# Column tiles in pairs, operands loaded in place, residual tiles one by one: a change to the FFN of a hybrid decoder step

## The chip, the cores and the metric

The kernel runs on one core of a Trainium2 chip. The metric is the device time of one execution in microseconds (us). The profile is that of one execution, with its time given beside its span.

## What is computed

The reference is one step of a decoder layer for 2048 prompt tokens and 32 sample tokens (width 1024): a mixer of differential attention and retention, its output added to the tokens, then a SwiGLU FFN (inner width 2816) and a final norm, all in float32. What the change touches is the FFN and the writing of its operands:

```
def swiglu(h, w_in_l, w_out_l):
    g, u = jnp.split(h @ w_in_l, 2, axis=-1)
    return (jax.nn.silu(g) * u) @ w_out_l
...
    xp = xp + swiglu(rms_norm(xp, norm_ffn_g[l], NORM_EPS), w_ffn_in[l], w_ffn_out[l])
...
y_prompt = rms_norm(xp, norm_final_g, NORM_EPS)
y_sample = rms_norm(xs, norm_final_g, NORM_EPS)
```

## The kernel before

**Arithmetic.** A float32 product is made of three matmuls: each operand is split into a high part (a cast on ACT, L122) and a low part (source minus high part on DVE, L123), and TensorE (PE) adds high times high, low times high and high times low. The FFN's block products use a scheme of seven products for a 2 by 2 block multiplication, with sums of blocks in place of the eighth. The products have the numbers 0, 4, 5, 6, 1, 2, 3, in the order in which they are run.

**Mixer's output.** For each tile of 128 tokens the output stage (`stats`, `weigh`, `finish`, `sums`, L957 to L1013) writes the residual x to DRAM (x2_d, which the profile calls x_d), norms and transposes the tile (ctp, L979), and writes blocks of it as xop_d: blocks 0, 1 and 3 directly (L993 to L996), blocks 4, 6, 5 and 2 after four sums of a pair of tiles on POOL (L1008 to L1013). SP issues these writes. xop_d[g][o] holds the operand of product o for token half g (g = 0, 1; 1024 tokens each). The sample tokens go to xs_d.

**FFN-in** (`ffn_in`, L1075 to L1233) runs over the token halves g, in each over eleven pairs of column tiles j, in each over the two tiles e of the pair.
- `operands(g)` (L1095) loads 28 blocks of 256 KB, four (k) for each product. A load goes into one of four staging buffers so0 to so3, and is split from there into the tiles xh and xl of that product and k. There is one such tile each, so those of g = 1 wait for the last product of g = 0 that reads them. POOL's sums at the end of a pair (L1215 to L1218) use the same four buffers.
- For each tile e SP loads 1 MB of w (L1178, two buffers, also used by w2); `weights` (L1109) makes four differences on POOL (wt) and splits seven halves into wh and wl, which have eight buffers each.
- `product` (L1133) runs 12 matmuls of 128 by 128 by 512 into one PSUM bank (fps, L1139). Seven banks go around, and four are taken for each e: products 0 and 1 share one, 4 and 2, 6 and 3, and 5 has its own.
- Between them ACT copies banks (c1, c5), DVE adds a bank to a line (L1191, L1194, L1203, L1207), and ACT applies silu.
- In g = 0 the sample tokens take part (`sample_in` L1148: sz, DVE's copy zs, then strips at L1167). They need xs, which POOL loads at L1089.
- At the end of a pair POOL makes four sums and writes seven blocks hop_d of 256 KB (L1221).
- In g = 1 `second` (L1235) follows: SP loads w2 (two rows of w_ffn_out, L1239), PE multiplies the sample tokens with it (sacc, L1243), and POOL writes four differences top_d (L1258).

**FFN-out** (`ffn_out`, L1260 to L1353) runs the seven products in the order 0, 1, 5, 4, 2, 6, 3, each over eleven j and eight PSUM banks p. `operands` (L1290) loads hop_d (512 KB, staging xr, three buffers) and a row of w_ffn_out or top_d (256 KB, wr, four) on SP and splits them into xh, xl, vh and vl, four buffers each; a j has 24 matmuls (L1305). The 16 residual tiles x (512 KB each) are loaded on POOL at L1278, before the products. At the end of product 0 the sample rows are loaded (xsr, L1351), added to ysum (L1352) and normed.

**What sets the order.** Each engine works through one queue in order, and so do the queues on which SP and POOL issue DMAs. The framework places each engine's instructions with a model of their times, so an instruction can stand elsewhere than the program's text has it. The pools of the FFN lie on one side of the on-chip memory: a tile of FFN-out may lie where tiles of FFN-in were, and then it waits for the last reader of those.

Of the kernel before, what the change touches and what calls it, by code (L numbers as in the profile page):

```python
# [11 lines left out]
F32 = mybir.dt.float32  # L12
F32R = mybir.dt.float32r
# [8 lines left out]
P = 128  # L22
# [23 lines left out]
class Step:  # L46
# [3 lines left out]
    def run(self):  # L50
        tc = self.tc
        with (
# [11 lines left out]
            self.xs_d = dram.tile([P, KT, NS], F32, name="xs_d")  # L64
            self.hop_d = [[dram.tile([P, 2, 512], F32, name=f"hop_d{j}_{o}") for o in range(7)] for j in range(NF // 2)]
# [822 lines left out]
    def out_rows(self, cr, ps, tiles, zps=None):  # L888
# [82 lines left out]
        def finish(t):  # L971
# [24 lines left out]
            nc.sync.dma_start(d[3][:, :, c], xt[:, half:])  # L996
            self.odd = (t, xt)

        def sums():
# [12 lines left out]
            for o, src in ((4, a22), (6, a21), (5, a11), (2, a12)):  # L1012
                nc.sync.dma_start(d[o][:, :, c], src)  # L1013
# [40 lines left out]
    def ffn(self):  # L1054
        tc, nc, a = self.tc, self.nc, self.a
        with ExitStack() as st:
# [8 lines left out]
            self.ysum = fs.tile([NS, D], F32, name="ysum")  # L1065
# [9 lines left out]
    def ffn_in(self):  # L1075
        nc, tc, a = self.nc, self.tc, self.a
        half = KT // 2
        with ExitStack() as st:
# [9 lines left out]
            xs = fx.tile([P, KT, NS], F32, name="xs")  # L1088
            nc.gpsimd.dma_start(xs, self.xs_d)  # L1089
            acc = None  # L1090

            def line(tag, bufs=1):
                return fw.tile([P, 512], F32, tag=tag, name=tag, bufs=bufs)

            def operands(g):  # L1095
                x = {}
                n = 0
                for o in (0, 4, 5, 6, 1, 2, 3):
                    for k in range(half):
                        r = line(f"so{n % 4}")  # L1100
                        n += 1
                        nc.sync.dma_start(r, self.xop_d[g][o][:, k, :])
# [6 lines left out]
            def weights(w):  # L1109
                wv = w.rearrange("p s k c -> p s (k c)")  # L1110
                w11, w21, w12, w22 = wv[:, 0, :512], wv[:, 0, 512:], wv[:, 1, :512], wv[:, 1, 512:]
                ws = {}

                def put(o, src):
                    h, l = self.halves(fw, src, 512, ("wh", "wl"), 8)
                    ws[o] = (h, l)

                tt = nc.gpsimd.tensor_tensor
                put(0, w11)
                t1, t2, t3, t4 = (line("wt", 4) for _ in range(4))  # L1120
                tt(t1, w12, w11, ALU.subtract)
                put(4, t1)
                tt(t2, w22, t1, ALU.subtract)
                put(5, t2)
                tt(t3, w22, w12, ALU.subtract)
                put(6, t3)
                put(1, w21)
                put(2, w22)
                tt(t4, w21, t2, ALU.subtract)
                put(3, t4)  # L1130
                return ws

            def product(o, bank, x, ws, first):  # L1133
                h, l = ws[o]
# [13 lines left out]
            def sample_in(f, w):  # L1148
# [11 lines left out]
                zs = fw.tile([P, 2 * P], F32, tag="zs", name="zs", bufs=1)  # L1160
# [9 lines left out]

            for g in range(2):
                x = operands(g)
                for j in range(NF // 2):
                    hh = []
                    for e in range(2):
                        f = j + e * (NF // 2)
                        w = fw.tile([P, 2, KT, P], F32, tag="w", name="w", bufs=2)
                        nc.sync.dma_start(w, a["w_ffn_in"][f].rearrange("s p k c -> p s k c"))  # L1178
                        ws = weights(w)
                        ba, bb, bc_, bd = (ring.tile() for _ in range(4))  # L1180
                        product(0, ba, x, ws, True)
# [340 lines left out]
```

## Time and profile before

| | us |
|---|---|
| median of three runs | 2728.57 (2726.32 to 2728.86) |
| profiled execution | 2728.34 |
| its span | 2726.6 |
| PE busy | 2616.8 (96%) |
| DVE busy | 1568.0 (58%) |
| ACT busy | 1061.8 (39%) |
| POOL busy | 950.8 (35%) |
| mean DMA rate | 152 GB/s |

A busy PE is not PE at its best: it counts as busy at the reduced clock too, so the granted clock is read beside it. The stages of the FFN are seen by PE's lines: L1153 and L1139 begin with FFN-in at about 1338 us, L1243 marks the second token half, L1305 begins at 2281 us and ends at 2713 us.

### The profile page before, as it was taken

The page shows a single profiled execution, that of the slowest core. Times are in us where ns is not written, and L with a number is a line of the kernel's source. Part 1 is how long each engine was busy: PE and PEld are TensorE (multiplying, and loading weights), DVE is VectorE, ACT ScalarE, POOL GpSimd, SP SyncE. Part 2 cuts the span into 40 slices and gives each one's busy share as a digit, 9 for nine tenths or more (in the row PEclk, how much of TensorE's full clock was granted, in tenths as well). Part 3 has the DMA queues.
Part 4 walks back from the last instruction along what each step waited for, and adds up shares of the span by engine and source line. Part 5 has one row for each costly group of instructions (what it writes and reads, how often), then busy time and mean ns, then how long its engine had stood idle before and what let it go on. Part 6 is the DMA issues. An engine that isn't in the chain of part 4 may idle for free. (4 is left out here: it accounts for less than half of the span.)

```text
span 2726.6 us, 35659 instructions
## 1 busy us (share of the span) xinstructions
PE 2616.8 (96%) x13180; PEld 2092.6 (77%) x13180; DVE 1568.0 (58%) x2296; ACT 1061.8 (39%) x2051; POOL 950.8 (35%) x991
## 2 busy tenths in 40 slices
PE   8999999999898999998899999979999999899998
PEld 7777788787566888887667777757888787688886
DVE  5554554543657677774375555547877874345364
ACT  4343343432556555653243333334332332332342
POOL 1000000011651122214246555546777774003121
PEclk9999999999999999999999999989999999899999
DMA  7436455364995455525442233245444447544463
GB/s 248 127 102 193 142 161 144 109 178 129 271 243 136 130 166 134 145 84 177 152 139 93 82 102 107 82 147 174 142 167 139 147 163 278 175 145 146 144 203 114
DMA packets 197550, 413.12 MB, mean 152 GB/s; under 512 B 20176, under 2 KB 84368, under 8 KB 197376
## 3 DMA queue, kind: packets, MB, share of 16 engines
q1 hardware_dynamic: 133568, 265.66, 30.7%
q0 software_dynamic: 54592, 140.98, 17.5%
q10 hardware_dynamic: 9216, 4.20, 0.6%
q8 instruction: 104, 1.70, 0.3%
q14 instruction: 70, 0.57, 0.1%
HBM read 287.82 MB, written 122.95 MB: 151 GB/s over the span
## 5 line engine op out<-in xcount | busy, mean ns | idle before, releaser
L1139 PE MATMUL fps<-xh,wh 128*128 128x512 f32 x1232 | 486.9, 398 | 20.0 <-ACT xh L122 19.6
L1139 PE MATMUL fps<-xl,wh 128*128 128x512 f32 x1232 | 483.3, 393 | 3.4 <-DVE xl L123 3.4
L1139 PE MATMUL fps<-xh,wl 128*128 128x512 f32 x1232 | 481.0, 391 | 0.0
L294 PE MATMUL z<-wh,xh 128*128 128x512 f32 x768 | 303.7, 397 | 7.7 <-ACT xh L188 7.7
L296 PE MATMUL z<-wl,xh 128*128 128x512 f32 x768 | 304.2, 397 | 0.0
L295 PE MATMUL z<-wh,xl 128*128 128x512 f32 x768 | 302.4, 394 | 0.0
L1139 PEld LDWEIGHTS fps<-xh,wh 128*128 128x128 f32 x1232 | 232.5, 189 | 89.9 <-ACT xh L122 25.3
L1139 PEld LDWEIGHTS fps<-xl,wh 128*128 128x128 f32 x1232 | 232.7, 189 | 57.0 <-DVE xl L123 9.3
L1139 PEld LDWEIGHTS fps<-xh,wl 128*128 128x128 f32 x1232 | 232.6, 189 | 49.3 <-issue 0.4
L123 DVE TENSOR_TENSOR wl<-wt,wh 128x512 fp32r<-128x512 f32 x176 | 218.4, 1246 | 77.7 <-ACT wh L122 73.1
L1305 PE MATMUL ops<-vh,xh 128*128 128x512 f32 x616 | 234.1, 391 | 12.7 <-ACT xh L122 10.6
L1305 PE MATMUL ops<-vh,xl 128*128 128x512 f32 x616 | 239.3, 391 | 0.0
L1305 PE MATMUL ops<-vl,xh 128*128 128x512 f32 x616 | 239.1, 390 | 0.0
L792 DVE TENSOR_REDUCE mx<-sp 128x1 f32<-128x1024 f32 (+4 forms) x192 | 168.7, 908 | 77.5 <-PE sp L791 76.9
L123 DVE TENSOR_TENSOR wl<-w,wh 128x512 fp32r<-128x512 f32 x132 | 161.2, 1232 | 87.9 <-ACT wh L122 87.9
L122 ACT CAST wh<-w 128x512 fp32r<-128x512 f32 x132 | 81.3, 621 | 304.6 <-PE fps L1139 170.5
L122 ACT CAST wh<-wt 128x512 fp32r<-128x512 f32 x176 | 109.1, 621 | 212.3 <-PE fps L1139 174.6
L123 DVE TENSOR_TENSOR wl<-wr,wh 128x1024 fp32r<-128x1024 f32 x96 | 117.3, 1223 | 106.7 <-ACT wh L122 94.4
L294 PEld LDWEIGHTS z<-wh,xh 128*128 128x128 f32 x768 | 145.2, 189 | 37.8 <-ACT xh L188 7.7
L296 PEld LDWEIGHTS z<-wl,xh 128*128 128x128 f32 x768 | 144.7, 188 | 31.9 <-issue 0.7
L295 PEld LDWEIGHTS z<-wh,xl 128*128 128x128 f32 x768 | 144.9, 189 | 31.1 <-issue 0.3
L123 DVE TENSOR_TENSOR vl<-wr,vh 128x512 fp32r<-128x512 f32 x77 | 58.3, 759 | 187.0 <-ACT vh L122 183.8
(307 smaller groups left out, 5002.8 us busy)
## 6 DMA issues: line engine op xcount, KB each, us to landing
wr<-w_in SPq DMA_DIRECT2D x96, 512.0 KB
w<-w_ffn_in SPq DMA_DIRECT2D x44, 1024.0 KB
xr<-hop_d SPq DMA_DIRECT2D x77, 512.0 KB
hop_d<-so POOLq DMA_DIRECT2D x88, 256.0 KB, 2.7
kst<-k_d POOLq DMA_DIRECT2D x36, 512.0 KB, 6.8
hop_d<-h POOLq DMA_DIRECT2D x66, 256.0 KB, 2.3
qd<-q_d POOLq DMA_DIRECT2D x64, 256.0 KB, 5.6
xop_d<-xt SPq DMA_DIRECT2D x56, 256.0 KB
```

Source lines behind the costliest of these rows:

```text
L122: nc.scalar.copy(hi, src)
L123: nc.vector.tensor_tensor(lo, src, hi.bitcast(F32), ALU.subtract)
L294: mm(z, h[:, j, c], wh[:, j], start=k == 0, stop=False)
L295: mm(z, l[:, j, c], wh[:, j], start=False, stop=False)
L296: mm(z, h[:, j, c], wl[:, j], start=False, stop=k == KT - 1)
L792: nc.vector.tensor_reduce(mx[:, c : c + 1], sp[:, :w], AX.X, ALU.max, negate=True)
L1139: nc.tensor.matmul(bank, w[:, c], v, start=first and k == 0 and n == 0, stop=k == half - 1 and n == 2, skip_group_check=True,)
L1305: nc.tensor.matmul(bank, x[:, c], w, start=first and n == 0, stop=end and n == 2, skip_group_check=True)
```

## The change

- The mixer's blocks xop_d are written by POOL's queue instead of SP's.
- FFN-in's operands are loaded into the xl tiles themselves, and xl is replaced in place by the low part. The staging buffers so are now POOL's alone. xs is loaded after the operands of g = 0 are asked for in the text.
- The two tiles e of a pair go side by side: both w are loaded, each product is run for e = 0 and then for e = 1, and the halves of the weights are made in that order. Six banks are taken for a pair; product 5 shares one with 6 and 3. The lines u2, sg and z21 are gone, their contents going into c1, u3 and h.
- `second` stands between products 6 and 1 instead of at the end of the pair.
- ysum goes through DRAM (ys_d). Small lines get a pool of their own (fe).
- In FFN-out the operands are loaded into xl in place, and xh, xl, vh and vl have five buffers. The residual tiles are loaded on SP, a pair of them behind each of the first eight operands of product 0. The sample rows are added and normed at product 5.

The core of the diff. Of FFN-in's loop only the new lines are shown; the old ones are in the listing above.

```
+    self.ys_d = dram.tile([NS, D], F32, name="ys_d")
...
-        nc.sync.dma_start(d[0][:, :, c], xt[:, :half])
-        nc.sync.dma_start(d[1][:, :, c], xt[:, half:])
+        nc.gpsimd.dma_start(d[0][:, :, c], xt[:, :half])
+        nc.gpsimd.dma_start(d[1][:, :, c], xt[:, half:])
...
-        nc.sync.dma_start(d[o][:, :, c], src)
+        nc.gpsimd.dma_start(d[o][:, :, c], src)
...
-    self.ysum = fs.tile([NS, D], F32, name="ysum")
...
+    fe = pool("fe", bufs=1)
...
     def operands(g):
         x = {}
-        n = 0
         for o in (0, 4, 5, 6, 1, 2, 3):
             for k in range(half):
-                r = line(f"so{n % 4}")
-                n += 1
-                nc.sync.dma_start(r, self.xop_d[g][o][:, k, :])
                 h = fx.tile([P, 512], F32R, tag=f"xh{o}{k}", name=f"xh{o}{k}")
                 l = fx.tile([P, 512], F32R, tag=f"xl{o}{k}", name=f"xl{o}{k}")
-                self.split(h, l, r)
+                nc.sync.dma_start(l.bitcast(F32), self.xop_d[g][o][:, k, :])
+                self.split(h, l, l.bitcast(F32))
                 x[o, k] = (h, l)
         return x
...
+        t1 = [line("wt", 4, fw) for _ in range(2)]
+        for e in range(2):
+            tt(t1[e], w12[e], w11[e], ALU.subtract)
+            put(4, e, t1[e])
+        t2 = [line("wt", 4, fw) for _ in range(2)]
+        for e in range(2):
+            tt(t2[e], w22[e], t1[e], ALU.subtract)
+            put(5, e, t2[e])
...
+    def load(j):
+        ww = []
+        for e in range(2):
+            w = fw.tile([P, 2, KT, P], F32, tag="w", name="w", bufs=2)
+            nc.sync.dma_start(w, a["w_ffn_in"][j + e * (NF // 2)].rearrange("s p k c -> p s k c"))
+            ww.append(w)
+        return ww
...
     for g in range(2):
+        ww = load(0)
         x = operands(g)
+        if g == 0:
+            xs = fe.tile([P, KT, NS], F32, name="xs")
+            nc.gpsimd.dma_start(xs, self.xs_d)
         for j in range(NF // 2):
+            if j:
+                ww = load(j)
+            ws = weights(ww)
+            ba, bc_, bd = ([ring.tile() for _ in range(2)] for _ in range(3))
+            c1, c5, h1, h2 = [], [], [], []
             for e in range(2):
+                product(0, e, ba[e], x, ws, True)
+                c1.append(line("c1", 2))
+                nc.scalar.copy(c1[e], ba[e])
+            for e in range(2):
+                product(4, e, bc_[e], x, ws, True)
+                c5.append(line("c5", 2))
+                nc.scalar.copy(c5[e], bc_[e])
                 if g == 0:
+                    z, zs = sample_in(ww[e])
+                    product(5, e, bd[e], x, ws, True)
+                    sample_mid(j + e * (NF // 2), z, zs)
+            for e in range(2):
+                if g:
+                    product(5, e, bd[e], x, ws, True)
+                add(c1[e], bd[e], c1[e], ALU.add)
+            u2 = c1
+            for e in range(2):
+                product(6, e, bd[e], x, ws, True)
+                u3 = line("u3", 2)
+                add(u3, bd[e], u2[e], ALU.add)
+                padd(c5[e], u3, c5[e], ALU.add)
             if g == 1:
                 if j == 0:
                     acc = psf.tile([P, 512], F32, tag="sz", name="sacc", bufs=1)
                 self.second(fw, line, j, acc)
+            sg = []
+            for e in range(2):
+                product(1, e, ba[e], x, ws, False)
+                sg.append(line("u3", 2))
+                nc.scalar.activation(sg[e], ba[e], AF.Silu)
+            for e in range(2):
+                product(2, e, bc_[e], x, ws, False)
+                h1.append(line(f"h{e}0"))
+                add(h1[e], bc_[e], u2[e], ALU.add)
+                add(h1[e], sg[e], h1[e], ALU.mult)
+            for e in range(2):
+                product(3, e, bd[e], x, ws, False)
+                h2.append(line(f"h{e}1"))
+                add(h2[e], bd[e], u2[e], ALU.add)
+                nc.scalar.activation(h2[e], h2[e], AF.Silu)
+                add(h2[e], h2[e], c5[e], ALU.mult)
+            h11, h12, h21, h22 = *h1, *h2
...
-        nc.scalar.copy(self.ysum[:, 512 * n : 512 * n + 512], z[:NS])
+        ys = line("u3", 2)
+        nc.scalar.copy(ys[:NS], z[:NS])
+        nc.gpsimd.dma_start(self.ys_d[:, 512 * n : 512 * n + 512], ys[:NS])
...
-    for p in range(8):
+
+    def residual(p):
         t0 = 2 * P * p
         for r, xs in ((t0, xa), (t0 + P, xb)):
             x = fz.tile([P, D], F32, name=f"x{len(xa) + len(xb)}")
-            nc.gpsimd.dma_start(x, self.x2_d[r : r + P, :])
+            nc.sync.dma_start(x, self.x2_d[r : r + P, :])
             xs.append(x)
-        us.append(fz.tile([P, 512], F32, name=f"u{p}"))
...
-        xr = fo.tile([P, 2, 512], F32, tag="xr", name="xr", bufs=3)
-        nc.sync.dma_start(xr, self.hop_d[j][o])
+        xh, xl = (fo.tile([P, 1024], F32R, tag=n, name=n, bufs=5) for n in ("xh", "xl"))
+        nc.sync.dma_start(xl.bitcast(F32), self.hop_d[j][o].rearrange("p g t -> p (g t)"))
...
-        x = self.halves(fo, xr.rearrange("p g t -> p (g t)"), 1024, ("xh", "xl"), 4)
-        return *x, *self.halves(fo, wr, 512, ("vh", "vl"), 4)
+        self.split(xh, xl, xl.bitcast(F32))
+        return xh, xl, *self.halves(fo, wr, 512, ("vh", "vl"), 5)
...
+            if o == 0 and j < 8:
+                residual(j)
+                us.append(fz.tile([P, 512], F32, name=f"u{j}"))
...
-        if o == 0:
-            xs = fo.tile([NS, D], F32, name="xsr")
-            nc.gpsimd.dma_start(xs, self.x2_d[S:, :])
-            padd(xs, self.ysum, xs, ALU.add)
+        if o == 5:
+            xs, ys = (fo.tile([NS, D], F32, name=n) for n in ("xsr", "ysr"))
+            nc.sync.dma_start(xs, self.x2_d[S:, :])
+            nc.sync.dma_start(ys, self.ys_d)
+            padd(xs, ys, xs, ALU.add)
             norm(xs, a["y_sample"], NS)
```

Three places of the order. First SP's queue from FFN-in to FFN-out: w and w2 are FFN-in's last weights, xr, xl and wr FFN-out's operands, x the residual tiles. Before:

```order
L1178 DMA w<-w_ffn_in 128x2x1024 x2
L1239 DMA w_19674<-w_ffn_out 128x1024 x2
L1292 DMA xr<-hop_d_0_90 128x1024
L1298 DMA wr<-w_ffn_out 128x512
L1292 DMA xr<-hop_d_0_97 128x1024
L1298 DMA wr<-w_ffn_out 128x512
```

And now, where the first two and the last two of the 16 rows of x are shown:

```order
L1179 DMA w<-w_ffn_in 128x2x1024 x2
L1263 DMA w_19340<-w_ffn_out 128x1024 x2
L1303 DMA x_19511<-x_d 128x1024
L1303 DMA x_19513<-x_d 128x1024
...
L1303 DMA x_19791<-x_d 128x1024
L1303 DMA x_19793<-x_d 128x1024
L1316 DMA xl<-hop_d_0_91 128x1024
L1322 DMA wr<-w_ffn_out 128x512
```

All 16 residual tiles, which were on POOL's queue, now stand on SP's ahead of the first operand, although the text has only two of them behind each operand.

Second, SP's queue at the change of the token half; so and xl are the targets of the operand loads, the number in xop_d's name belongs to the product. Before:

```order
L1178 DMA w<-w_ffn_in 128x2x1024 x20
L1102 DMA so_15972<-xop_d_0_82 128x512
L1178 DMA w<-w_ffn_in 128x2x1024
L1102 DMA so_15996<-xop_d_4_86 128x512
L1102 DMA so_16020<-xop_d_5_87 128x512
L1239 DMA w_16434<-w_ffn_out 128x1024 x2
L1102 DMA so_16044<-xop_d_6_88 128x512
L1102 DMA so_16068<-xop_d_1_83 128x512
```

And now:

```order
L1179 DMA w<-w_ffn_in 128x2x1024 x20
L1099 DMA xl_15852<-xop_d_0_82 128x512
L1099 DMA xl_15857<-xop_d_0_82 128x512
L1099 DMA xl_15862<-xop_d_0_82 128x512
L1099 DMA xl_15867<-xop_d_0_82 128x512
L1179 DMA w<-w_ffn_in 128x2x1024
L1099 DMA xl_15872<-xop_d_4_86 128x512
L1099 DMA xl_15877<-xop_d_4_86 128x512
```

The loads of the second half follow the order of the products now, with the weights of the next pair in between, and w2 stands behind all of them.

Third, PE at the entry of the FFN, from the last transpose of the mixer (ctp) on; sz is the sample product, strips its second step, fps a block product. Before:

```order
L979 MATMUL ctp<-ident,xn 128x128 x8
L1139 MATMUL fps<-xh_12109,wh 128x512 x2
L1139 MATMUL fps<-xl_12110,wh 128x512
L1139 MATMUL fps<-xh_12109,wl 128x512
L1139 MATMUL fps<-xh_12115,wh 128x512
```

And now:

```order
L980 MATMUL ctp<-ident,xn 128x128 x8
L1157 MATMUL sz<-w,xs 32x256 x8
L1171 MATMUL sz<-strips,zs 128x32 x2
L1157 MATMUL sz<-w,xs 32x256 x8
L1171 MATMUL sz<-strips,zs 128x32 x2
L1143 MATMUL fps<-xh_12112,wh 128x512 x2
```

The sample products of both tiles of the pair now stand ahead of the first block product; before, the first of them stood 13 rows behind it.

More of the change, by code (lines that the diff above doesn't have):

```diff
@@ L1087, in ffn_in, with line @@
             ring = _Ring(psg, psf)
[L1088 to L1093, printed above, removed]
+            def line(tag, bufs=1, pool=fe):
+                return pool.tile([P, 512], F32, tag=tag, name=tag, bufs=bufs)
             def operands(g):
                 x = {}
-                n = 0
                 for o in (0, 4, 5, 6, 1, 2, 3):
@@ L1118, in weights @@
                 tt = nc.gpsimd.tensor_tensor
[L1119 to L1130, printed above, removed]
@@ L1131, in weights @@
-                return ws
-            def product(o, bank, x, ws, first):
-                h, l = ws[o]
+                v = [w.rearrange("p s k c -> p s (k c)") for w in ww]
+                w11, w21 = [x[:, 0, :512] for x in v], [x[:, 0, 512:] for x in v]
+                w12, w22 = [x[:, 1, :512] for x in v], [x[:, 1, 512:] for x in v]
+                for e in range(2):
+                    put(0, e, w11[e])
+                t1 = [line("wt", 4, fw) for _ in range(2)]
+                for e in range(2):
+                    tt(t1[e], w12[e], w11[e], ALU.subtract)
+                    put(4, e, t1[e])
@@ new lines, in weights @@
+                t2 = [line("wt", 4, fw) for _ in range(2)]
+                for e in range(2):
+                    tt(t2[e], w22[e], t1[e], ALU.subtract)
+                    put(5, e, t2[e])
+                t3 = [line("wt", 4, fw) for _ in range(2)]
+                for e in range(2):
+                    tt(t3[e], w22[e], w12[e], ALU.subtract)
+                    put(6, e, t3[e])
+                for e in range(2):
+                    put(1, e, w21[e])
+                for e in range(2):
+                    put(2, e, w22[e])
@@ L1135, in product @@
+                for e in range(2):
+                    tt(t2[e], w21[e], t2[e], ALU.subtract)
+                    put(3, e, t2[e])
+                return ws
+            def product(o, e, bank, x, ws, first):
+                h, l = ws[o, e]
                 for k in range(half):
@@ L1169, in sample_mid @@
                 nc.vector.tensor_tensor(self.hs[:, f, :], t[:, 1, :], self.hs[:, f, :], ALU.mult)
+            def load(j):
[5 more added lines that the diff above has]
+                return ww
+            acc = None
+            add, padd = nc.vector.tensor_tensor, nc.gpsimd.tensor_tensor
@@ L1212, in ffn_in @@
-                    h11, h21, h12, h22 = hh
-                    so = [line(f"so{n}") for n in range(4)]
-                    tt = nc.gpsimd.tensor_tensor
-                    tt(so[0], h21, h22, ALU.add)
-                    tt(so[1], so[0], h11, ALU.subtract)
-                    tt(so[2], h11, h21, ALU.subtract)
-                    tt(so[3], h12, so[1], ALU.subtract)
-                    d = self.hop_d[j]
-                    for o, src in enumerate((h11, h12, so[3], h22, so[0], so[1], so[2])):
-                        nc.gpsimd.dma_start(d[o][:, g, :], src)
+                    if j:
+                        ww = load(j)
@@ L1250, in second @@
         w11, w12, w21, w22 = w[:, 0, :512], w[:, 0, 512:], w[:, 1, :512], w[:, 1, 512:]
-        t = [line("wt", 4) for _ in range(4)]
+        t = [line("wt", 4, fw) for _ in range(4)]
         tt = nc.gpsimd.tensor_tensor
```

66 lines of the change are left out of this document (20 added, 46 removed).

## The prediction

> **What bounds the kernel now.** First the page: the busy line and the chain that ended last say which engine to follow.
>
> ```profile
> PE 2616.8 (96%) x13180; PEld 2092.6 (77%) x13180; DVE 1568.0 (58%) x2296; ACT 1061.8 (39%) x2051; POOL 950.8 (35%) x991
> PE ops L1305 14%; PE fps L1139 14%; DMA so<-xop_d 1%; DMA x<-x_d 1%; DVE xl L123 0%; PE sacc L1243 0%; DMA xsr<-x_d 0%; DMA w<-w_ffn_in 0%; ACT xh L122 0%; DMA hop_d<-so 0%; DVE wl L123 0%; DVE y L1287 0%; POOL ss L118 0%; POOL xsr L1352 0%; POOL so L1218 0%
> ```
>
> TensorE carries the span. The change leaves the number of its matmuls alone, so only the time in which it stands still, or runs at a reduced clock, can be won or lost. The chain names three such places: so<-xop_d, x<-x_d and xsr<-x_d. A table by stage shows how large they are. Its columns are the stretch, its length, busy time and instructions of PE, PEld, DVE, ACT and POOL, the granted clock, DMA share and GB/s.
>
> ```profile
> 1330.00:1400.00 70.00, 56.63 (x234) 38.77 (x233) 42.79 (x59) 31.82 (x57) 23.52 (x21) 0.90 0.51 164
> 1400.00:1815.00 415.00, 414.74 (x2075) 329.69 (x2073) 224.14 (x301) 132.14 (x242) 233.50 (x210) 1.00 0.29 99
> 1815.00:1872.00 57.00, 36.51 (x132) 24.76 (x133) 33.31 (x41) 21.40 (x38) 23.66 (x22) 0.85 0.61 204
> 1872.00:2055.00 183.00, 183.00 (x819) 147.80 (x818) 143.76 (x129) 61.43 (x107) 138.79 (x133) 1.00 0.41 146
> 2277.00:2295.00 18.00, 15.87 (x66) 11.90 (x67) 11.95 (x13) 10.47 (x14) 10.73 (x16) 1.00 0.73 251
> 2295.00:2318.00 23.00, 23.00 (x103) 19.06 (x102) 3.83 (x5) 2.82 (x4) 5.05 (x10) 1.00 1.03 407
> 2318.00:2330.00 12.00, 1.41 (x8) 0.83 (x6) 0.17 (x2) 2.14 (x4) 2.89 (x2) 0.64 0.49 189
> 2330.00:2335.00 5.00, 5.00 (x12) 3.94 (x13) 5.00 (x5) 3.06 (x5) 0.00 (x0) 0.50 0.45 139
> 2331.00:2709.00 378.00, 378.00 (x1661) 312.77 (x1660) 178.96 (x198) 128.76 (x177) 59.89 (x43) 0.99 0.47 152
> ```
>
> A matmul at full clock starts every 378.00/1661 = 0.2276 us; at the clock of 0.50 twelve take 5 us, so each restart costs 5 − 12 × 0.2276 = 2.3 us beside the idle time. Both long steady stretches have no idle PE. What is left are three places; the rows behind the table are of the first and the last of them.
>
> ```profile
> L1139 PE MATMUL fps<-xh,wh 128*128 128x512 f32 x59 | 24.2, 430 | 2.6 <-ACT xh L122 2.6
> 2275.10 1.06 PE L1243 MATMUL sacc<-w,hs 128*32 128x512 f32 x8
> ```
>
> - **A, entry of the FFN** (1330 to 1400): 13.4 us idle and a clock of 0.90. Of the 234 rows 175 are products, three groups like the one above: 39.8 us. The sample products and strips (3.5) and the mixer's last rows (2) make it about 45 us of work in 70, a loss of about 24.5 us.
> - **B, change of the token half** (1815 to 1872): 132 rows, of them 8 sacc at 1.06/8 = 0.13 us. 124 × 0.2276 + 1.0 = 29.2 us of work in 57, a loss of 27.8 us.
> - **D, from FFN-in to FFN-out** (2277 to 2335): 18 − 66 × 0.2276 = 3.0, then nothing at 2295 to 2318, then 12 − 8 × 0.2276 = 10.2, then 2.3, and 0.8 us between the last sacc's end and 2277: 16.3 us.
>
> **A.** Timelines of POOL, SP and PE say what was late (start, duration, engine, line, what), two rows of PE's waits give the total and the longest, and one group the length of a copy (total, mean in ns).
>
> ```profile
> 1345.34 1.26 POOL L1011 TENSOR_TENSOR xt<-xt 128x512 f32<-128x512 f32 x1
> 1346.55 0.61 POOL L1089 DMA_DIRECT2D xs<-xs_d  x1
> 1342.59 4.55 SPq L1013 DMA_DIRECT2D xop_d<-xt  x4
> 1347.24 11.40 SPq L1102 DMA_DIRECT2D so<-xop_d  x10
> 1349.03 1.93 PE L1153 MATMUL sz<-w,xs 128*32 128x256 f32 x14 [5.63 <-DMA xs<-xs_d]
> PE ctp L979 <- DVE xn L969: 4.2, 1, 4.2
> PE fps L1139 <- ACT xh L122: 2.6, 2, 2.2
> L1161 DVE COPY zs<-sz 128x256 f32<-128x256 f32 x20 | 8.3, 414 | 0.0
> ```
>
> The load of xs stood behind POOL's four sums, and SP could not load operands while it waited to issue the sums' writes at L1013. Now xs is issued on POOL ahead of the last sums, the writes have left SP, and the 28 operand loads follow there without a gap. The 5.63 us go, with them one restart (2.3), and I take 2 of the 2.6 us for xh. Against that PE now begins with both sample products and waits for DVE's zs copy between them (0.4 us each), which I cost at 0.5. The 4.2 us that the last transpose waits for xn stay. Sum −9.5; bounds −4 (the 5.63 alone, less 1.6 us of zs waits, two copies each way) and −13 (all idle time but the 4.2, which is 9.2, and nearly two restarts). POOL pays for the 56 writes with some 0.6 us each, ahead of its loads in the mixer. The nearest row is another store that it issues there; the page's line of POOL's busy tenths (68 us a slice, the FFN from the twentieth on) has it free for at least four tenths of each slice, so I take nothing, and up to 5 us for the range.
>
> ```profile
> 1332.67 0.62 POOL L960 DMA_DIRECT2D x_d<-xres  x1 [7.13 <-DVE xres L955]
> POOL 1000000011651122214246555546777774003121
> ```
>
> **B.** The chain of waits in order of time (start, length, what) is a loop of load, cast, subtract:
>
> ```profile
> 1825.13 3.49 DMA so<-xop_d
> 1828.65 0.63 ACT xh L122
> 1829.30 0.70 DVE xl L123
> ...
> 1830.51 3.18 DMA so<-xop_d
> ```
>
> Four staging buffers, shared with POOL's sums, let a load start only when the split of four loads ago is over. The loads now go into the xl buffers themselves, and such a buffer is free as soon as its product of the last column pair is done: product 0 within 5.5 us (2 × 12 × 0.2276), while its successor is wanted some 38 us later. A load of 3 to 4 us disappears in that. What is late next is DVE, which has the same number of subtracts to make in less time:
>
> ```profile
> L123 DVE TENSOR_TENSOR wl<-wt,wh 128x512 fp32r<-128x512 f32 x79 | 72.3, 915 | 50.1 <-ACT wh L122 50.0
> L123 DVE TENSOR_TENSOR wl<-w,wh 128x512 fp32r<-128x512 f32 x60 | 66.7, 1112 | 37.9 <-ACT wh L122 37.9
> L123 DVE TENSOR_TENSOR xl<-so,xh 128x512 fp32r<-128x512 f32 x25 | 22.6, 918 | 25.3 <-ACT xh L122 25.3
> ```
>
> A pair of the first half costs DVE 224.14/10 = 22.4 us, a pair of the second half about 143.76/183 × 39.2 = 30.8, and the 28 splits 28 × 0.918 = 25.7: together 78.9 us in the 41.5 + 39.2 = 80.7 us of PE's two pairs around the change. That is full, not over full, and the eight weight buffers give some slack: I leave 4 us of loss (0 to 12). Two loads of w stand among the 28 and make SP wait for a weight buffer; product 5's operands are wanted 11 us after product 0's, which covers it. B is −24, bounds −28 and −16.
>
> **D.** Here the change has a price. In the trace SP fetched the first operands of FFN-out some 15 us before FFN-in ended, and POOL the residual tiles:
>
> ```profile
> 2261.60 0.33 SPq L1292 DMA_DIRECT2D xr<-hop_d  x1
> ...
> 2265.18 1.09 SPq L1298 DMA_DIRECT2D wr<-w_ffn_out  x2
> L1278 POOL DMA_DIRECT2D x<-x_d x16: 527/528/552, 2289.6 to 2313.7; - x16
> 2297.29 18.32 DMA x<-x_d
> 2315.89 9.47 DMA xsr<-x_d
> 2325.50 2.34 POOL xsr L1352
> 2329.01 0.94 ACT xh L122
> ```
>
> PE ran on those until 2318, while the DMA moved 407 GB/s, at a share of 1.03: that is the ceiling. Then it starved behind the sample rows' norm, which took ACT's place in line and waited for xsr. The norm moves to product 5, and that wait goes. But in SP's new order all 16 residual tiles stand ahead of the first operand (the rows are in the section on the change). x0 to x3 find room before the last matmul of FFN-in; x4 to x15 lie over the operands of its last products, so they and everything behind them start when FFN-in ends. Then the DMA has to carry 12 tiles of 0.524 MB (15.5 us at 407 GB/s), what is left of x2 and x3 (2.6), POOL's last seven hop_d blocks and gfin (7 × 0.262 + 0.524 = 2.36 MB, 5.8) and the first operand pair (0.786 MB, 1.9), before ACT can cast (0.94): 26.8 us idle, 2.3 of restart, 29.1. After that a column needs 24 × 0.2276 = 5.5 us and its 0.786 MB 1.9: no further wait. D goes from 16.3 to 29.1, +12.8; I take +12.5. Bounds: +5, where half of the twelve tiles get room earlier, and +18, five or six more than the sum, about a third of the 18.32 us that an x tile took to land in the crowded DMA.
>
> [...]
>
> **Steady pairs.** The row is DVE's add on a product's bank in the second half (total, mean in ns).
>
> ```profile
> L1191 DVE TENSOR_TENSOR u<-fps,c 128x512 f32<-128x512 f32 x10 | 6.8, 681 | 0.2
> ```
>
> The same product of both column tiles now runs back to back; the numbers of matmuls, splits, adds and sums stay. With six banks instead of eight, product 6 waits for DVE's add on product 5's bank; the order has rows of other products in between, and such an add takes 0.68 us, so it is covered by one product of 12 × 0.2276 = 2.7 us. The load of w2 is nearer to its user: it can start only when the buffer of the pair's first w is free, after products 0 and 4 (10.9 us), and sacc comes after product 5 (16.4 us). That leaves 5.5 us for the splits behind product 4 and 1 MB, which at 407 GB/s takes 2.6 at best. I take +2 in all, 0 to +15.
>
> **Sum.** From the profiled execution's 2728.34 (span 2726.6): −9.5 − 24 + 12.5 + 2 = −19, 2709.3. The median of the runs is 0.2 above it. Forecast **2709 us**. The tail behind the last matmul isn't touched.
>
> **The rivals.**
> - *Slower: w2 stalls every pair of the second half.* PE takes its rows in order, so a sacc without w2 holds back all products behind it. For: 5.5 us is little, DVE and POOL are busy for 79% and 76% of 1872 to 2055, and the next w needs the buffer after w2. Against: 1 MB takes 2.6 us if the DMA is free, whose share was 0.41. With 2.7 us in each of 11 pairs it costs 30: −9.5 − 24 + 12.5 + 30 = +9, **2737 us**. It decides from 21 + 5.5 = 26.5 us, so 2.4 us a pair.
> - *The residual tiles cost nothing.* If they find room in time, or operands pass between them, D keeps its 16 us: −9.5 − 24 + 0 + 2 = −31.5, **2697 us**. Against it stand SP's order and the ceiling of 407 GB/s; for it, that I infer x4 to x15's room from overlaps and not from a wait.
> - *DVE is the bound at B.* 78.9 of 80.7 us is a mean; what queues in the wrong order makes PE wait. With 16 us left of B's loss instead of 4, and 4 in the steady pairs: −9.5 − 12 + 12.5 + 4 = −5, **2723 us**.
>
> **How the numbers follow.** A measurement of this kernel can tell about 0.2%, 5.5 us, from no change. Forecast 0.62 (own range 2697 to 2720), slower rival 0.12, residual tiles free 0.12, DVE 0.14. Faster: 0.62 + 0.12 and about a quarter of DVE's, 0.78; same: the rest of that, 0.10; slower 0.12. The range runs from 2695, below the rival with free tiles, to 2731, beyond DVE's; only the slower rival and stray ends lie outside.
>
> **What would show it.** Right: no idle PE between the halves beyond a few microseconds, with xl as the loads' target; xs landed before the last transpose; 25 to 30 us in which PE waits for xh after the last fps matmul, with sixteen x loads on SP ahead of the first xl<-hop_d and the DMA near 407 GB/s. Wrong: an idle of under 15 us there; waits of sacc on w<-w_ffn_out or of fps on wl in each pair; PE waiting on xl for over 10 us at the change.

## The result and the profile after

The changed kernel takes 2754.23 us in the median of four runs (2746.98 to 2756.09), the kernel before 2727.7 in four. The ratio is 1.0093, 95% interval 1.0073 to 1.0112: slower by 0.9%, where 0.7% faster was forecast. The profiled execution took 2752.57 us with a span of 2750.8, 24.2 more than before.

The busy line and the chain that ended last, of the changed kernel:

```profile
PE 2631.7 (96%) x13180; PEld 2098.5 (76%) x13180; DVE 1512.9 (55%) x2296; ACT 1065.6 (39%) x2051; POOL 1003.8 (36%) x1032
PE fps L1143 28%; PE ops L1329 15%; PE sacc L1267 1%; PE sz L1157 1%; DVE wl L124 1%; DMA x<-x_d 1%; DMA w<-w_ffn_out 0%; DMA w<-w_ffn_in 0%; DMA xl<-hop_d 0%; PE sz L1171 0%; DVE xl L124 0%; DVE y L1311 0%; DMA xs<-xs_d 0%; ACT xh L123 0%; DVE h L1232 0%
```

so<-xop_d is gone from the chain, and TensorE (PE) is busy for 15 us longer with the same 13180 matmuls. The waits of PE (waiting line, on what, us in total, times, longest) in the changed kernel:

```profile
PE sp L789 <- ACT p L807: 28.3, 18, 4.9
PE ops L1329 <- ACT vh L123: 27.0, 1, 27.0
PE ctp L980 <- DVE xn L970: 10.7, 3, 4.4
PE cz L948 <- DVE xres L956: 8.5, 4, 3.8
...
PE sacc L1267 <- DMA w<-w_ffn_out: 5.0, 3, 2.5
```

The 27.0 us before FFN-out were forecast at 26.8. SP's queue (start, duration, line, what, count) of the changed kernel has what the order promised, all residual tiles in a row and the first operand behind them:

```profile
2281.63 21.66 SPq L1303 DMA_DIRECT2D x<-x_d  x16
2304.63 0.32 SPq L1316 DMA_DIRECT2D xl<-hop_d  x1
```

The chain (start, length, what) goes through both, up to the casts that PE waits for:

```profile
2290.16 14.45 DMA x<-x_d
2304.62 0.02 issue
2304.63 10.21 DMA xl<-hop_d
...
2314.95 1.04 ACT xh L123
2315.99 0.53 ACT vh L123
```

Three of the other waits, sp, ctp and cz, stand ahead of the FFN, where the forecast put nothing; sp is part of the attention, ctp and cz of the mixer's output. In the kernel before they were shorter:

```profile
PE sp L788 <- ACT p L806: 22.1, 18, 3.6
PE ctp L979 <- DVE xn L969: 7.8, 2, 4.2
PE cz L947 <- DVE xres L955: 2.9, 3, 2.0
```

The rows of the mixer's transposes, ctp (count, durations in ns, first and last start), of the kernel before and of the changed one:

```profile
L979 PE MATMUL ctp<-ident,xn x136: 221/273/477, 897.2 to 1337.4; 128*128 128x128 f32 x128, 32*128 32x32 f32 x8
```

```profile
L980 PE MATMUL ctp<-ident,xn x136: 221/273/474, 906.4 to 1359.0; 128*128 128x128 f32 x128, 32*128 32x32 f32 x8
```

So 21.6 us were lost before the FFN began. Four rows of the table by stage of the changed kernel, from the change of the half to FFN-out (columns as in the prediction):

```profile
1820.00:1860.00 40.00, 37.80 (x159) 28.74 (x158) 30.37 (x39) 16.12 (x30) 29.73 (x25) 0.96 0.48 171
1860.00:1900.00 40.00, 37.46 (x156) 28.38 (x155) 23.51 (x23) 11.52 (x21) 31.36 (x30) 0.96 0.45 157
1980.00:2060.00 80.00, 80.00 (x344) 62.49 (x343) 55.28 (x52) 25.14 (x44) 61.55 (x58) 1.00 0.41 142
2288.00:2316.00 28.00, 1.55 (x4) 0.22 (x2) 1.14 (x2) 2.72 (x5) 8.49 (x12) 0.57 1.01 389
```

From 1980 to 2060 us, in the second token half, PE shows no idle time at a clock of 1.00, yet it gets through 344 rows in 80 us; before it was 819 in 183, or 358 in 80. That is a loss that neither the busy time nor the waits show.

I divide both executions at points that can be found in every trace: the last transpose's start, the end of the first pair of FFN-in, the first matmul of the last pair of the first half (j = 10, the 1681st fps matmul), the last fps product, and the last ops product.

| stretch | before | changed | difference | forecast |
|---|---|---|---|---|
| to the last transpose | 1337.4 | 1359.0 | +21.6 | 0 |
| from there over the first pair (to the 169th fps matmul) | 61.2 | 54.0 | −7.2 | −9.5 |
| the pairs between | 374.4 | 374.4 | 0 | 0 |
| j = 10 of the first half to the last fps product | 501.8 | 500.0 | −1.8 | −22 (−24 and +2) |
| from there to the last ops product | 438.3 | 450.9 | +12.6 | +12.5 |
| tail | 13.6 | 12.6 | −1.0 | 0 |

The sum is the +24.2 of the span. Two stretches come near their forecasts, and two hold 42 of the 43 us between forecast and result: the mixer and the second half. The −1.8 of the second half is itself made of two parts: the two pairs around the change of the half (from j = 10 to the 169th product matmul of the second half) take 85.9 us instead of 109.2, a gain of 23.3, and the ten pairs that follow take 414.1 instead of 392.6, a loss of 21.5.

### The profile page after: what moved, and what is told of

It is laid out like the page before. It is cut to its first block, busy times and chain, and to the rows that moved or that the text cites. A ratio compares the mean times of both kernels' runs of the same rounds, so it can differ in the third digit from the quotient of the medians.

```text
span 2750.8 us, 35630 instructions
## 1 busy us (share of the span) xinstructions
PE 2631.7 (96%) x13180; PEld 2098.5 (76%) x13180; DVE 1512.9 (55%) x2296; ACT 1065.6 (39%) x2051; POOL 1003.8 (36%) x1032
## 4 chain that ended last, share of the span: by engine, by line
PE 45%; DMA 2%; DVE 2%; issue 1%; ACT 0%; POOL 0%; SPq 0%; POOLq 0%; DVEq 0%; ACTq 0%
PE fps L1143 28%; PE ops L1329 15%; PE sacc L1267 1%; PE sz L1157 1%; DVE wl L124 1%; DMA x<-x_d 1%; DMA w<-w_ffn_out 0%; DMA w<-w_ffn_in 0%; DMA xl<-hop_d 0%; PE sz L1171 0%; DVE xl L124 0%; DVE y L1311 0%; DMA xs<-xs_d 0%; ACT xh L123 0%; DVE h L1232 0%
## 5 line engine op out<-in xcount | busy, mean ns | idle before, releaser
L1329 PE MATMUL ops<-vh,xh 128*128 128x512 f32 x616 | 239.8, 392 | 27.0 <-ACT vh L123 27.0
L124 DVE TENSOR_TENSOR xl<-xl,xh 128x1024 fp32r<-128x1024 f32 (+1 forms) x133 | 143.2, 1094 | 219.7 <-ACT xh L123 219.2
L793 DVE TENSOR_REDUCE mx<-sp 128x1 f32<-128x1024 f32 (+4 forms) x192 | 168.4, 908 | 85.9 <-PE sp L792 66.0
L124 DVE TENSOR_TENSOR wl<-w,wh 128x512 fp32r<-128x512 f32 x132 | 150.2, 1148 | 111.5 <-ACT wh L123 111.0
L124 DVE TENSOR_TENSOR wl<-wt,wh 128x512 fp32r<-128x512 f32 x176 | 192.8, 1099 | 30.7 <-ACT wh L123 30.7
L123 ACT CAST xh<-xl 128x1024 fp32r<-128x1024 f32 (+1 forms) x133 | 113.2, 869 | 231.5 <-DMA xl<-hop_d 214.9
L123 ACT CAST wh<-wt 128x512 fp32r<-128x512 f32 x176 | 109.2, 621 | 197.0 <-PE fps L1143 170.2
```

The lines of the kernel that those rows point to most:

```text
L123: nc.scalar.copy(hi, src)
L124: nc.vector.tensor_tensor(lo, src, hi.bitcast(F32), ALU.subtract)
L793: nc.vector.tensor_reduce(mx[:, c : c + 1], sp[:, :w], AX.X, ALU.max, negate=True)
L1329: nc.tensor.matmul(bank, x[:, c], w, start=first and n == 0, stop=end and n == 2, skip_group_check=True)
```

## The experiments

The theory names three separate costs. POOL's queue pays for the xop_d writes in the mixer; sacc, torn into several places of a pair, costs PE time at each; the residual tiles hold up the first operands of FFN-out. Rivals: the mixer's time drifts by chance; w2 is late; the DMA's ceiling (389 GB/s at a share of 1.01 from 2288 to 2316 us, in the table above) would cost the same wherever the residual tiles are issued. Each run is compared with runs of the kernel before on the same chip (median 2724.9 to 2725.5 for the first eight, 2735.4 for the last two), so times of different chips aren't compared; stretches come from the traces.

### The writes back on SP

```
-                nc.gpsimd.dma_start(d[o][:, :, c], src)
+                nc.sync.dma_start(d[o][:, :, c], src)
```

and the same at blocks 0, 1 and 3.

> The changed kernel with one part undone: the mixer's xop_d writes are issued by SP again. In the trace of the changed kernel the last transpose of the mixer begins at 1359.0 us, 21.6 later than before; 8.6 of these are lost by 820 us, where no engine's order differs, 13 behind it, where the writes are. Theory 'POOL's queue' (56 writes delay the loads, sums and norm steps behind them): the last transpose comes some 13 us earlier, near 1346, and since SP stands still again at the entry some 3 to 6 us are given back there; time about 2745. If the writes cause the early part too (through the DMA), near 1338 and 2736. Rival 'drift' (the mixer's engines meet by chance, and the writes have no part): the last transpose stays at 1355 to 1360 and the time at 2752 to 2758. The rest, the idle of 27 us before FFN-out and the second half's 458 us, stays by both.

Measured: 2731.19 us, ratio 1.0015 (1.0001 to 1.0029) to the kernel before. The last transpose is back:

```profile
L980 PE MATMUL ctp<-ident,xn x136: 221/273/477, 895.5 to 1338.1; 128*128 128x128 f32 x128, 32*128 32x32 f32 x8
```

That is the number of the case in which the writes cause the early part too, but not for that reason: 10.9 of the 20.9 us lie ahead of the first transpose, where the orders of both kernels are the same. The next section takes this up.

The entry took 54.3 us against 54.0. The move of the writes to POOL had gained nothing there; it exchanged one wait for another. PE's waits at the entry in the changed kernel, and its wait for xs in this run:

```profile
PE sz L1157 <- DMA xs<-xs_d: 4.7, 1, 4.7
PE fps L1143 <- ACT xh L123: 0.8, 1, 0.8
```

```profile
PE sz L1157 <- DMA xs<-xs_d: 0.6, 1, 0.6
```

Here the wait for xh is 5.4 us: SP, busy with the writes, begins the operand loads 9.9 us after the last transpose. In the changed kernel it begins them 12.3 us ahead of it, but then xs is late. Its load is issued 1.3 us ahead of the last transpose in both kernels; here it landed after 2.3 us, with the DMA at 23 to 66 GB/s, and in the changed kernel PE could start on it only 6.4 us after its issue, with the DMA at 386 to 395 GB/s. That the operand loads hold up xs is my reading; no run separates the two.

So the wait for xs, which step A had counted as gone, was still there, and the 7.2 us come from elsewhere. PE's idle time in the stretch fell only from 9.2 to 7.3 us; its busy time for the same 211 rows fell from 52.0 to 46.7. The likely source is the place of the sample products. In the kernel before with operands in place (further down) the first block product starts 15.8 us after the last transpose, and the 169th 45.8 us behind that; in this run it is 14.3 and 40.0, with the sample products of both tiles done while PE waits for the operands anyway. No run moved them alone.

### The kernel before with the writes on POOL

The same four lines in the other direction, in the kernel before.

> The kernel before with one part of the change: the mixer's xop_d writes are issued by POOL. Theory 'POOL's queue': the last transpose of the mixer, at 1337.4 us before, comes 10 to 20 us later; SP no longer stands still for the writes at the entry of the FFN, which gives some 3 to 5 back: 2735 to 2745. Rival 'drift': the last transpose stays within 3 us of 1337.4 and the time at 2722 to 2728, the gain at the entry alone.

Measured: 2743.29 us, ratio 1.0057 (1.003 to 1.0085). Last transpose 1350.8, 13.4 later; entry 62.5 against 61.2, nothing given back. The two runs agree in direction. By the medians the price is 18.4 us here (2743.29 less 2724.87; 8 to 23 by the interval). The run above and the one with the residual tiles on POOL further down differ by 17.5 (2748.64 less 2731.19), but 6.8 us of their profiles' difference lie behind the entry, so that pair doesn't measure the writes alone. POOL's waits between 830 and 1335 us in this run hold rows that the kernel before doesn't have:

```profile
POOL xop_d L996 <- DVE xt L982: 31.1, 6, 13.9
POOL xop_d L994 <- DVE xt L982: 26.2, 3, 13.4
POOL xop_d L993 <- ACT xt L984: 25.0, 3, 10.5
```

POOL stands before a write until its tile is ready, and behind it stand the next tile's norm steps (nss, css) and the residual's store. Other waits of POOL shrink in return (x_d for xres from 94.1 to 50.4 us), so these rows don't add up to the price. Which of the steps behind a write carries the cost wasn't tried alone. In the changed kernel the writes themselves took 0.82 us each in the median at four blocks of seven:

```profile
L1014 POOL DMA_DIRECT2D xop_d<-xt x32: 719/824/1038, 984.2 to 1372.0; - x32
```

Over all twelve profiles (the two kernels and ten runs) the stretch from the eleventh tile's transposes to the last one's is 93.6 to 98.0 us where SP writes (six) and 101.1 to 104.7 where POOL does (six); from the first tile's to the eleventh's 343.3 to 345.9 against 346.1 to 349.8. The means differ by 7.4 and 2.9, which is 10.3 of the 18.4 us; where the rest lies isn't shown. The first transpose, ahead of which no engine's order differs, comes at 890.4 to 906.4 us, with no difference between the two groups: of the changed kernel's 21.6 us, 9.2 lie there, and I take them for chance in that one execution: the five other kernels with the writes on POOL have it at 895.5 to 902.0. 'POOL's queue' is shown, for the output stage; 'drift' fits the part ahead of the first transpose.

### w2 at the pair's end

```
-                    if g == 1:
...
-                        self.second(fw, line, j, acc)
                     sg = []
...
                         nc.gpsimd.dma_start(d[o][:, g, :], src)
+                    if g == 1:
...
+                        self.second(fw, line, j, acc)
```

> The changed kernel with one part undone: the step with w2 and sacc stands at the end of a pair again, so that the four sacc matmuls of a pair stand together on PE (in the changed kernel they stand in two or three places of a pair). Theory 'column groups': the four fill different column groups of the array and run at the same time when they follow each other; each place costs about 1.08 us beyond the matmuls. The second token half, 458.3 us in the changed kernel and 444.2 before with its first pair cut short, should take 11 x 39.3 = 432 us, with the waits for w2 (5.0 us) and their restarts gone too: 24 to 26 us less, about 2729. Rival 'w2 late': only the waits and restarts count (8 us), the places don't: 2746. If w2 is late wherever it stands, the waits move and sacc waits as before: 2738.

Measured: 2782.35 us, ratio 1.0215 (1.019 to 1.0241); 537.5 us from j = 10 to the last fps product, pairs of 45 to 46 us. None of the three forecasts held. sacc ran in one place (eight rows in 1.04 us), but PE now waited for weights (first row; total, times, longest), and the chain shows why (the wait came in ten of the eleven pairs):

```profile
PE fps L1143 <- ACT wh L123: 38.6, 10, 4.1
```

```profile
2042.06 1.04 PE sacc L1267 x8
2043.09 0.02 SPq L1179
2043.12 0.04 issue
2043.16 6.06 DMA w<-w_ffn_in
2049.22 0.02 issue
2049.24 0.63 ACT wh L123
2049.86 0.04 issue
2049.91 0.79 PE fps L1143
```

w2 shares two buffers with the two w of a pair. Since the pairs hold both w at once, the next pair's second w waits for w2's last reader; with sacc at the pair's end it starts when it is wanted. So pairs and w2 at the end don't go together with two buffers, and the place between products 6 and 1 is what the pairs call for.

### sacc in one place

```
+                m = nc.tensor.matmul(
...
+                self.tc.keep_in_program_order(m)
```

and the same at the first matmul of product 1 behind it, so that no other row comes between the four. One sacc shows as two rows.

> The changed kernel with one part altered: the four sacc matmuls of a pair are held in one place on PE, between products 6 and 1 as the text has them; w2 keeps its buffers and its place. Theory 'column groups' (each separate place costs 1.08 us, 27 places become 11): 16 x 1.08 = 17 us less, and the waits for w2 (5.0 us with two restarts of 2) shrink, since sacc comes two products later; from the last pair of the first half to the end of FFN-in 476 to 484 us against 500 in the changed kernel; time 2728 to 2738. Rival 'w2 is late': sacc waits for w2 in each pair at its one place, as the weights did in the run with w2 at the pair's end; 495 us or more, time 2745 to 2755.

Measured: 2720.69 us, ratio 0.9981 (0.9963 to 0.9999); 477.1 us from j = 10 to the last fps product against 500.0. Counted again, the changed kernel has 26 places, not 27, so 15 go. The rows of PE's timeline (start, length, count), first of the changed kernel, in one pair, then of this run:

```profile
1935.72 1.05 PE L1267 MATMUL sacc<-w,hs 128*32 128x512 f32 x2
1944.18 1.06 PE L1267 MATMUL sacc<-w,hs 128*32 128x512 f32 x6
```

```profile
1927.22 1.06 PE L1269 MATMUL sacc<-w,hs 128*32 128x512 f32 x8
```

Two rows take as long as six or eight: the four sacc fill 32 columns each of the array, and they run at the same time if they stand together. The trace shows it in the starts: in one place of this run the first rows of the four lie within 0.02 us, and the second rows follow 0.45 us later, again together. 15 × 1.08 = 16.2 us and the 5.0 us of waits for w2 make 21.2 of the 22.9. The other 1.7 fit PE's slow start behind those waits, by my estimate: in the changed kernel two rows of sacc took 1.57 and 1.91 us right behind the two waits of over 2 us, with a clock of 0.82 (1845 to 1850) and 0.76 (1890 to 1895). Pairs take 39.3 us again, as before the change. 'Column groups' is shown, and 'w2 is late' holds for about a fifth, the 5.0 us of waits.

### Residual tiles on POOL, and in turn on SP

```
-                    nc.sync.dma_start(x, self.x2_d[r : r + P, :])
+                    nc.gpsimd.dma_start(x, self.x2_d[r : r + P, :])
```

> The changed kernel with one part undone: the residual tiles are loaded on POOL's queue again, so that SP's first FFN-out loads are operands. Theory 'residual tiles ahead of the operands': the 27.0 us in which PE waits for the first operand go, and with the sample rows now at product 5 the 10.6 us of before do not come back; from the last product of FFN-in to the end 438 - 10 - 2 = 426 us or less against 450.9 in the changed kernel: 22 to 25 us less, about 2731. Rival 'DMA ceiling': the residual tiles' 8.4 MB take 21 us of the DMA wherever they are issued, the operands share it and PE starves a few microseconds per column: 10 to 14 us less, about 2742.

Measured: 2748.64 us, ratio 1.0084 (1.0051 to 1.0116), and 452.1 us from the last fps to the last ops product: no gain. SP did load five operands from 2252 us on, 30 us before FFN-in ended, and PE waited 29.6 us all the same. The chain of this run:

```profile
2286.35 7.81 DMA x<-x_d
2294.16 0.28 issue
2294.45 9.91 DMA x<-x_d
2304.36 0.28 issue
2304.64 0.53 POOL x L1303
2305.17 0.02 issue
2305.18 1.27 POOL so L1242
...
2308.25 0.49 POOL hop_d L1247
2308.74 4.74 DMA hop_d<-so
```

The residual loads now stood on POOL ahead of the last pair's sums and hop_d writes, and PE's first halves came only after a write out of so had landed. My reading is that the first high part xh lies over the lines so0 and so1 that these writes read. A second wait had the place of the first, so this run tells neither theory. The next one left them on SP, but in the text's order:

```
-                    nc.sync.dma_start(x, self.x2_d[r : r + P, :])
+                    tc.keep_in_program_order(nc.sync.dma_start(x, self.x2_d[r : r + P, :]))
```

> The changed kernel with one part altered: the residual loads stay on SP but are held at their place in the text, two behind each operand, so that the first operands are loaded before FFN-in ends and POOL's last sums and hop_d writes stand behind nothing. Theory 'residual tiles ahead of the operands': from the last product of FFN-in to the last of FFN-out 426 to 432 us against 450.9; time 2729 to 2737. Rival 'the weights' halves lie over the sums' lines' (what PE waited for with the residual tiles on POOL): vh waits for hop_d to be read out, some 5 to 8 us behind FFN-in's end with nothing ahead of it; 434 to 440 us, time 2737 to 2745. If the DMA ceiling alone decides: 445 or more.

Measured: 2728.75 us, ratio 1.0017 (1.0004 to 1.003); 438.3 us, PE waited 14.8. That is the middle case: the residual tiles' price falls by 12.6, and the writes out of so are what is late next. The time itself lies under that case's range: in the profile the mixer ended 9 us earlier than in the changed kernel's, and the second half was 4 us shorter.

### All three, and the high part moved

The writes on SP, sacc in one place and the residual loads in turn, by the edits above, in one kernel:

> The changed kernel with the three costs taken away at once: xop_d written by SP, sacc in one place, the residual loads in turn with the operands. If the costs add up: the mixer as before (last transpose near 1337), the entry 54, 476 to 484 from the last pair of the first half to the end of FFN-in, 426 to 440 from there to the last product: 2683 to 2702, some 1% under the kernel before. If they hide one another (sacc's waits or DVE's load come back elsewhere): 2705 to 2720.

Measured: 2697.4 us, ratio 0.9895 (0.9873 to 0.9917). Last transpose 1341.4, entry 55.4, 478.2, 437.3: by the stretches, each part keeps what it gained alone. What PE waits for before FFN-out is now a write out of so:

```profile
2258.32 6.63 DMA hop_d<-so
2264.95 0.92 ACT xh L123
```

This last wait was tried by giving the norm's tiles y their place first:

```
+            fo.tile([P, D], F32, tag="y", name="y", bufs=3)
             gfin = fz.tile([P, D], F32, name="gfin")
```

> The run with three parts mended, and one more: the norm's output tiles y get their place in FFN-out's pool first, so that the first high parts xh no longer lie over the lines so0 and so1 of FFN-in, whose hop_d writes are the last. Theory 'place': the 14.9 us in which PE waited for the first halves at the start of FFN-out were a wait for the writes out of so (the chain had hop_d<-so 6.63 right ahead of the cast); from the last product of FFN-in to the last of FFN-out 422 to 429 us against 437.3; time 2683 to 2690 against 2697. Rival 'DMA ceiling': residual tiles, hop_d and operands still share about 400 GB/s there, and the first column starves behind them; 433 to 438 us, time 2693 to 2698.

Measured: 2686.15 us, ratio 0.9833 (0.981 to 0.9855), 423.2 us from the last fps to the last ops product. The wait for the first halves has shrunk to

```profile
PE ops L1333 <- ACT vh L123: 2.2, 1, 2.2
```

from 14.9. The 423.2 us lie in the case of 'place' (422 to 429), 9.8 us under that of 'DMA ceiling' (433 to 438). This version beats both kernels, by 1.7% the one before.

### The kernel before with one or two parts

```
-                        nc.sync.dma_start(r, self.xop_d[g][o][:, k, :])
...
-                        self.split(h, l, r)
+                        nc.sync.dma_start(l.bitcast(F32), self.xop_d[g][o][:, k, :])
+                        self.split(h, l, l.bitcast(F32))
```

> The kernel before with one part of the change: FFN-in's operands are loaded into the xl tiles, without staging; no pairs, nothing else. Theory 'staging': the loss of 27.8 us at the change of the half goes whatever the order of the products is, and a part of the entry's: from the last pair of the first half to the end of FFN-in 474 to 480 us against 501.8; time 2695 to 2703. Rival 'pairs': the second half's operands come free early enough only with the pairs' order (product 0 of both tiles first); without it the operands are freed one tile later and 8 to 15 us of the loss stay: 482 to 490, time 2708 to 2715.

Measured: 2709.9 us, ratio 0.9949 (0.9932 to 0.9966); 485.8 us from j = 10 to the last fps product, 16 less than before, and the entry as before (61.6). By the stretch and the time it is the rival's case. In the two pairs around the change of the half loads in place alone give 89.2 us (89.1 in the next run) for 109.2, and with the pairs' order as well, sacc together, it is 80.9: the order adds some 8 us to 20. At the entry the theory's gain did not come; PE waited 15.4 us for xh in one piece.

Then the sample rows' norm at product 5 as well (`if o == 5:`), without the rest of the change:

> The kernel before with two parts of the change: FFN-in's operands loaded in place, and the sample rows added and normed at product 5 instead of product 0 (residual tiles stay on POOL, single column tiles). Theory 'norm in the way': the 10.0 us in which PE waited for xh behind the sample rows' norm go, with a restart of 2; from the last product of FFN-in to the last of FFN-out 427 to 430 us against 439.8 in the run with the operands alone: 2697 to 2700. Rival 'DMA ceiling': the operands were late anyway behind the residual tiles, and another wait of 6 to 10 us takes the place of the norm's: 2705 to 2710.

Measured: 2717.98 us, ratio 0.9938 (0.9918 to 0.9957), so no more than the part alone; 438.0 us, and PE waited 10.6 for xh as before. ACT's timeline shows why:

```profile
2318.34 1.05 ACT L1283 ACTIVATE y<-xsr 32x1024 f32<-32x1024 f32 x1 [18.87 <-POOL xsr L1350]
2319.30 0.18 ACT L1283 ACTIVATION_READ_ACCUMULATOR y<-xsr 32x1 f32 x1
2319.39 1.03 ACT L122 CAST xh<-xr 128x1024 fp32r<-128x1024 f32 x1
```

The norm was written later and still stood ahead of the casts in ACT's queue, waiting for xsr: the framework had put it back. Neither theory was tested.

## Why the prediction was wrong

- **What bounds it**: right that TensorE carries the span, but "only the time in which it stands still, or runs at a reduced clock, can be won or lost" left out a third way, work that PE does one after the other instead of side by side (eight rows of sacc in 1.06 us together, two in 1.05).
- **A**: near in size (−7.2 for −9.5), wrong in the mechanism, so the size is largely luck. "The 5.63 us go": they didn't, PE still waited 4.7 us for xs. Taking the writes off SP brought the first operand load earlier (12.3 us ahead of the last transpose for 9.9 behind it) and xs later (6.4 us after its issue for 2.3); with the writes back on SP it is the same 54 us (54.3). The sample products ahead of the first block product, which A counted as a cost of 0.5, are the likely gain.
- **A's last step, the writes' cost on POOL**: this failed. It read "has it free for at least four tenths of each slice, so I take nothing, and up to 5 us for the range". The runs put it at 18.4 us by the medians of the one clean pair, 10.3 of them (7.4 and 2.9) in the two stretches of the output stage. POOL's engine was free and its queue was not: busy for 36% of the changed kernel's span, POOL waited up to 13.9 us in front of a write for its tile (xop_d at L997, 28.4 us in five waits between 830 and 1360 us). The share said nothing of what stood behind such a write, and the norm of the next tile stood there, among others. I had priced the issue, 0.6 us, and not the wait, although the listing shows POOL's work in the same loop.
- **B**: right. The two pairs around the change of the half gained 23.3 us in the changed kernel and 28.3 with sacc together (80.9 for 109.2), −24 forecast. The margin was misjudged: DVE was reckoned at 78.9 of 80.7 us, and with sacc together it was busy for 54.4 of 80.9, so the 4 us left for it weren't needed.
- **D**: right in the wait and its size, 27.0 us for 26.8, +12.6 for +12.5. The terms fell otherwise: the first operand, counted at 1.9 us behind the tiles, took 10.21 from its issue, and the tiles ahead of it less. One part of the picture was missing: behind the residual tiles a second wait, for the writes out of so, would have come at 15 us.
- **Steady pairs**: this failed. "the numbers of matmuls, splits, adds and sums stay", +2: they do, but four sacc of 32 columns cost what one costs (1.06 us for eight rows, 1.05 for two) only when they stand together, and the framework spread them over two or three places of a pair. The ten pairs behind the change lost 21.5 us; holding sacc together won back 22.9 in the whole half, of which 5.0 were waits for w2. It could have been seen: the kernel before has eight rows of sacc in 1.06 us, which I quoted and divided by eight.
- **The rivals**: the slower one named the right instruction and came near the time (2737 for 2754), but not the mechanism: w2 made sacc wait three times, not in every pair. None of the three rivals had the mixer in it.
- **The sum**: from the forecast's −19 the mixer moves the profile by 21.6 us, the second half by 20.2 (−1.8 for −22), A by 2.3 and the tail by −1.0, to +24.2. What stays open: 9.2 us of the mixer's 21.6 lie ahead of the first transpose, where the other profiles show only chance, yet the median of the four runs is no lower than the profiled one.

## What to carry over

Before a DMA is moved to a queue that looks free, look at what its tile waits for and at what stands behind it on the new queue: here POOL's waits in front of the writes came to 25.0 to 31.1 us in each of three rows, where the forecast had priced the issue alone, at 0.6 us a write. The four sacc of 32 columns each took 1.06 us together and one of them alone 1.05, and holding them together won back 22.9 us, 5.0 of them waits for w2: where a scheduler may place such matmuls, hold them together. And where buffers are enlarged or loads moved, ask which earlier tile's place the first new tile takes: the wait for the writes out of so (PE stood for 14.9 us, and for 2.2 with the places changed) came from places in memory, not from data.

## What the runs showed of the hardware

- Two, six and eight rows of matmuls with 128 rows and 32 columns of weights took 1.05 to 1.06 us, at a clock of 1.00 in the changed kernel (1934 to 1950 us). In a place of eight, with sacc held in one place, the first four rows started within 0.02 us of each other, and the other four 0.45 us later.
- The load of xs (128 KB) landed 2.3 us after its issue with the DMA at 23 to 66 GB/s (the run with the writes on SP), and PE could use it only 6.4 us after its issue with the DMA at 386 to 395 GB/s (the changed kernel).
- With the same order of instructions on all five engines ahead of it, the first transpose came at 890.4 to 906.4 us in twelve profiles, and the kernel before took 2718.5 to 2741.4 us in 51 runs on more than one chip. On one chip alone it was 2718.5 to 2735.1 in 36 runs. What makes the difference wasn't traced; it is as large as the effect of most single edits here, so medians of several runs and stretches of the traces are needed beside each other.
